# Attention's operands: loads two or three units ahead, splits one unit later, four load slots

## The chip, the cores and the metric

The kernel runs on one core of a Trainium2 chip. The metric is the device time of one execution in microseconds (us); the median of several runs is given. The engines are PE (TensorE, matrix products), ACT (ScalarE), DVE (VectorE), POOL (GpSimd) and SP (SyncE), which issues all the DMA transfers here. Each engine takes its instructions in the order in which they stand in its queue; an instruction that waits holds all behind it.

## The reference

Two layers of a diffusion backbone over 1024 latent tokens and 256 context tokens. Each layer projects the normed input once, runs latent attention and a two-way gated delta rule side by side, joins both in one output projection, and ends in a squared-ReLU MLP. The change lies in attention, whose core is this:

```python
def mla_attend(q, k, v):
    ...
    def block(qi):
        s = jnp.einsum('bqhd,bkhd->bhqk', qi, k).astype(jnp.float32) * scale
        p = jax.nn.softmax(s, axis=-1).astype(v.dtype)
        return jnp.einsum('bhqk,bkhd->bqhd', p, v)

    attn_l = mla_attend(q, jnp.concatenate([kc, k], axis=1), jnp.concatenate([vc, v], axis=1))
    ...
    if not last:
        attn_c = mla_attend(qc, kc, vc)
```

There are 8 heads with 96 query and key columns and 64 value columns, all in float32. The context tokens' own attention is left out in the last layer.

## The kernel before, in words

Each layer has three stages. Stage 1 projects the input and writes queries, keys and values to DRAM (tensors qd, kd, vd). Stage 2 runs attention and the delta rule together. Stage 3 does the output projection and the MLP. To keep float32 precision, products are made of three: every operand is held as a high part (the value rounded to the engine's float32r format) and an exact remainder, and `mm3` (lines 313 to 315) adds high by high, low by high and high by low.

In stage 2 the work of attention is cut into units of 256 queries of one head: the context block (b = 0, one unit, first layer only), and two latent blocks (b = 1, 2) of two units each, called half 0 and 1. Layer 0 has 40 units and layer 1 has 32; one more step drains the last unit. `front` makes a unit's scores, takes them out of their bank with their maximum (DVE, `keep`), and applies the exponential (ACT, line 896, two per unit). It then sends the reciprocal sums through DRAM (rinv out, rb back). `back` transposes the exponentials (PE, pt), splits them into high part ph (ACT, line 927) and remainder pl (DVE, line 928), multiplies them by the values (PE, o, line 916), scales the result (POOL, ob, waiting for rb) and stores it (cat). The unit i's front and the unit i - 1's back are interleaved by the string PATTERN, and steps of the delta rule (products g, line 984, with their loads v, kt, kT, qT, QK, A and B) are laid between units.

A head's operands come by `parts`: for each chunk of 512 columns a load from DRAM into a slot raw (SP, line 831; three slots), a cast to the high part (ACT, line 832: kh, v, qh), and a subtraction for the remainder (line 834: on DVE for the first loads of a layer, on POOL after that). The keys of a head are three chunks, the values two, the queries of a block one. `load` and `loadq` are called at the start of the front that first needs the values.

The order of the instructions on each engine is not that of the source: a scheduler fixes it when the program is built. It takes the instructions by priority, which is the order of the source, as soon as its own model of time says that their operands and slots are ready. So a later head's load may be drawn ahead of earlier work. `tc.issue_after(ins)` holds those instructions of a block that run on the engine of `ins` behind `ins` in that engine's queue.

Of the kernel before, what the change touches and what calls it, by code (L numbers as in the profile page):

```python
# [46 lines left out]
# columns of the constant table  # L47
C_ID, C_M0, C_M1, C_ONE, C_W = 0, 128, 256, 384, 512
# and the part of it that is needed once
# [24 lines left out]
def host_layout(inp):  # L74
# [16 lines left out]
    # tiles of output columns: q 4, k 4, v 4, misc, kv_a, q_a 2, z 4  # L91
# [4 lines left out]
    # the rotary columns: first halves of all heads, second halves of all heads  # L96
# [19 lines left out]
class K:  # L116
# [13 lines left out]
    # ---------------------------------------------------------------- set-up  # L130
# [24 lines left out]
    def side(self, l):  # L155
        """The ends of the memory for the features and weights, and for the rest; layers swap them."""
        self.msd, self.osd = ("right", "left") if l % 2 else ("left", "right")
# [8 lines left out]
    def start(self, mmp, pjp, tpp, stp):  # L166
        """Modulation of the first norm, the first norm, and the first two output tiles, as the features come."""
        nc, io, cst = self.nc, self.io, self.cst
        with ExitStack() as es:
# [12 lines left out]
            # features and weights are queued behind the modulation's weights  # L182
# [73 lines left out]
    # ---------------------------------------------------------------- adaLN  # L256
    def ada_tile(self, l, m, vs, sp, width, other=()):
        """Column m of the modulation; the vectors in other go by way of Pool and ACT and want their sum()."""
# [17 lines left out]
    def ada_sum(self, l, v, m):  # L276
        """Eight columns that came by way of Pool and ACT, from their halves and the bias."""
# [4 lines left out]
    def load_sc(self, sp):  # L282
        """silu(c) and silu(c_ctx) on all partitions."""
        self.sc_b = []
        for v in range(2):
            t = sp.tile([P, D], F32, name=f"scr{v}")
            self.nc.sync.dma_start(t, self.scd[v].partition_broadcast(P))
            self.sc_b.append(t)

    def gain(self, l, j, vs):  # L290
        """(1 + scale) * gain of norm j."""
# [5 lines left out]
    # ---------------------------------------------------------------- weights  # L297
    def wload(self, src):
        """A [128, 1024] weight from DRAM as its float32r high part and exact remainder."""
# [17 lines left out]
    # ---------------------------------------------------------------- norms  # L317
    def rstat(self, sq, n, denom, stp, rbp=None):
        """rsqrt(mean + eps) over partitions of the [128, n] squares (list added), as PSUM [128, n] rows."""
# [17 lines left out]
    def norm_mod(self, xs, rb, b, l, which, pool):  # L337
        """Modulated RMSNorm of block b (8 tiles [128, n]) into the high and low parts of h."""
# [22 lines left out]
    # ---------------------------------------------------------------- stage 1  # L361
    def stage1(self, l, last):
        """Input projection, short conv, gates, chunk preparation, latent attention's projections."""
# [8 lines left out]
        # the solves may go on into the next stage  # L372
# [59 lines left out]
        def conv_tile(m, blocks, it=None):  # L432
            """Projection, short conv, twice the silu."""
# [65 lines left out]
        def first():  # L499
            """The first two output tiles, side by side, while the norm goes on."""  # L500
# [72 lines left out]
    def kpe(self, l, it, sp, tpp):  # L573
        """Rotary key part of all heads, and the gate columns by token."""
# [40 lines left out]
    def gates(self, l, stp):  # L615
        """Per-token scalars of both directions, [128 tokens, direction, tile, head]."""
# [45 lines left out]
        # the squares are of twice the features  # L662
# [24 lines left out]
    # ---- latent attention's low-rank parts  # L687
# [6 lines left out]
    def lowrank(self, raw, b, g, sp, stp):  # L694
        """RMSNorm of the low-rank features of block b, as high and low parts."""
# [27 lines left out]
    def kv_proj(self, l, raw, sp, mmp, stp):  # L723
        """Keys (but for the rotary part) and values of all heads, to DRAM as high and low parts."""
# [20 lines left out]
    def q_proj(self, l, raw, sp, mmp, stp):  # L745
# [3 lines left out]
        # the scale of the scores  # L749
# [31 lines left out]
    # ---------------------------------------------------------------- stage 2  # L781
    def stage2(self, l, last):
        dr = self.dr
        es = ExitStack()
        # what the first scores need, and then the first steps, lies where the stage before ends first
# [706 lines left out]
```

## Time and profile before

| | |
|---|---|
| median of 3 runs | 3950.51 us (3946.8 to 3952.6) |
| span of the profiled execution, first to last instruction | 3929.9 us |
| PE busy | 3517.4 us (90% of the span) |
| DVE busy | 2134.2 us (54%) |
| POOL busy | 1516.0 us (39%) |
| ACT busy | 1459.3 us (37%) |
| mean granted TensorE clock | 0.937 of full speed |

The profile shows one execution. Busy time is the time in which an engine executes an instruction; the sum over engines is larger than the span, since they work side by side. An engine that is idle waits for a releaser, which the profile names. SP's issues are not counted as busy time; its waits are listed on request.

### The profile page before, as it was taken

What the parts mean: (1) busy time and instruction counts of PE and PEld (TensorE: products, weight loads), DVE (VectorE), ACT (ScalarE), POOL (GpSimd) and SP (SyncE); (2) the same over time, 40 slices, a digit from 0 to 9 for tenths busy, and PEclk for the clock granted to TensorE, in tenths of its full rate; (3) what the DMA queues carried; (4) which work ended last, traced back from release to release, by engine and by line L of the source; (5) the groups of instructions that cost most, each with busy time, mean ns of one, the idle gap of its engine ahead of it and who ended that gap; (6) DMA issues with size and microseconds to landing.
All of it is one profiled execution on the core that took longest, in us unless ns stands there. A gap on an engine that the chain in (4) does not pass through costs nothing.

```text
span 3929.9 us, 52618 instructions
## 1 busy us (share of the span) xinstructions
PE 3517.4 (90%) x19001; PEld 2992.1 (76%) x19001; DVE 2134.2 (54%) x4080; ACT 1459.3 (37%) x3156; POOL 1516.0 (39%) x1358
## 2 busy tenths in 40 slices
PE   8789977887887898999999978888889899999998
PEld 4668766787776777888888757767788788888887
DVE  5157855565769995333333627776667533333334
ACT  4334355565633111121112524336666531222122
POOL 3124864433354232232223313675533352333232
PEclk8899987898998899999999979989899899999999
DMA  5343465535353352111111334454653511111111
GB/s 186 91 136 116 139 149 94 112 93 95 77 199 102 129 180 81 43 44 38 38 33 43 102 94 132 144 147 109 125 101 81 132 57 46 52 51 49 44 54 54
DMA packets 335892, 372.52 MB, mean 95 GB/s; under 512 B 126849, under 2 KB 226577, under 8 KB 333969
## 3 DMA queue, kind: packets, MB, share of 16 engines
q1 hardware_dynamic: 335632, 369.18, 34.3%
q8 instruction: 149, 2.44, 0.3%
q14 instruction: 111, 0.90, 0.1%
HBM read 280.65 MB, written 88.42 MB: 94 GB/s over the span
## 4 chain that ended last, share of the span: by engine, by line
PE 57%; DVE 13%; DMA 12%; issue 5%; ACT 4%; POOL 3%; SPq 1%; POOLq 0%; DVEq 0%; ACTq 0%
PE f2ps L313 6%; PE f2ps L314 6%; PE f2ps L315 6%; PE fps L314 6%; PE fps L315 6%; PE fps L313 6%; DVE adaj L272 3%; DMA raw<-kd 3%; PE g L984 3%; PE o L916 3%; PE pt L924 2%; DVE cacc L444 2%; DVE A L1427 2%; DMA rinv<-rinv 2%; DMA adaw<-w_adaT 1%
## 5 line engine op out<-in xcount | busy, mean ns | idle before, releaser
L308 POOL TENSOR_TENSOR wlo<-wraw,whi 128x1024 fp32r<-128x1024 f32 (+1 forms) x190 | 462.3, 2441 | 1217.8 <-ACT whi L307 1217.8
L1304 DVE SCALAR_TENSOR_TENSOR x<-f2ps,mod,x 128x512 f32<-128x512 f32 (+1 forms) x648 | 440.9, 689 | 353.3 <-PE f2ps L315 353.1
L307 ACT CAST whi<-wraw 128x1024 fp32r<-128x1024 f32 (+1 forms) x190 | 195.6, 1046 | 1008.0 <-PE f2ps L314 692.7
L313 PE MATMUL f2ps<-ah,whi 128*128 128x512 f32 (+1 forms) x1296 | 474.4, 371 | 31.4 <-DVE x L1304 27.2
L314 PE MATMUL f2ps<-al,whi 128*128 128x512 f32 (+1 forms) x1296 | 478.5, 370 | 0.8 <-DVE al L1293 0.8
L313 PE MATMUL fps<-hh,whi 128*128 128x512 f32 (+1 forms) x1288 | 471.3, 368 | 8.8 <-ACT hh L351 8.8
L315 PE MATMUL f2ps<-ah,wlo 128*128 128x512 f32 (+1 forms) x1296 | 477.4, 369 | 0.0
L314 PE MATMUL fps<-hl,whi 128*128 128x512 f32 (+1 forms) x1288 | 474.1, 368 | 0.0
L315 PE MATMUL fps<-hh,wlo 128*128 128x512 f32 (+1 forms) x1288 | 472.9, 368 | 0.0
L1293 DVE TENSOR_TENSOR al<-relu,ah 128x256 fp32r<-128x256 f32 (+1 forms) x161 | 111.5, 699 | 512.9 <-POOL relu L1292 512.9
L313 PE MATMUL mm<-hh,whi 128*128 128x512 f32 (+1 forms) x880 | 333.1, 380 | 35.0 <-ACT craw L430 22.1
L314 PE MATMUL mm<-hl,whi 128*128 128x512 f32 (+1 forms) x880 | 331.4, 377 | 3.6 <-DVE hl L352 2.1
L315 PE MATMUL mm<-hh,wlo 128*128 128x512 f32 (+1 forms) x880 | 327.6, 374 | 0.8 <-POOL wlo L308 0.8
L928 DVE TENSOR_TENSOR pl<-pt,ph 128x512 fp32r<-128x512 f32 x328 | 222.2, 686 | 194.7 <-ACT ph L927 182.1
L313 PEld LDWEIGHTS f2ps<-ah,whi 128*128 128x128 f32 x1296 | 248.2, 192 | 74.4 <-DVE x L1304 29.9
L313 PEld LDWEIGHTS fps<-hh,whi 128*128 128x128 f32 x1288 | 243.7, 190 | 49.1 <-ACT hh L351 9.1
L314 PEld LDWEIGHTS f2ps<-al,whi 128*128 128x128 f32 x1296 | 248.7, 192 | 40.7 <-DVE al L1293 1.0
L315 PEld LDWEIGHTS f2ps<-ah,wlo 128*128 128x128 f32 x1296 | 248.4, 192 | 40.1
L314 PEld LDWEIGHTS fps<-hl,whi 128*128 128x128 f32 x1288 | 244.0, 189 | 40.1 <-POOL hl L357 0.3
L315 PEld LDWEIGHTS fps<-hh,wlo 128*128 128x128 f32 x1288 | 243.9, 189 | 39.8
L924 PE MATMUL pt<-ctab,p 128*128 128x128 f32 x1312 | 219.9, 287 | 32.9 <-ACT p L896 12.7
L1292 POOL TENSOR_TENSOR relu<-relu 128x256 f32<-128x256 f32 (+1 forms) x161 | 159.5, 996 | 225.2 <-ACT ah L1291 209.7
(287 smaller groups left out, 7520.6 us busy)
## 6 DMA issues: line engine op xcount, KB each, us to landing
wraw<-w_ff SPq DMA_DIRECT2D x128, 512.0 KB
adaw<-w_adaT SPq DMA_DIRECT2D x160, 256.0 KB
wraw<-w_in SPq DMA_DIRECT2D x40, 512.0 KB
QK<-QK SPq DMA_DIRECT2D x72, 256.0 KB
A<-A SPq DMA_DIRECT2D x40, 256.0 KB
v<-vtd SPq DMA_DIRECT2D x40, 256.0 KB
kt<-ktd SPq DMA_DIRECT2D x40, 256.0 KB
kT<-kTd SPq DMA_DIRECT2D x36, 256.0 KB
```

Of the source, the lines that this page charges most:

```text
L272: nc.vector.tensor_tensor_reduce(out=j, in0=w, in1=self.sc_b[v][:, s], op0=ALU.mult, op1=ALU.add, scale=1.0, scalar=acc if i else self.bad ...
L307: nc.scalar.copy(hi[:, :n], raw[:, :n])
L308: nc.gpsimd.tensor_tensor(lo[:, :n], raw[:, :n], hi[:, :n].bitcast(F32), op=ALU.subtract)
L313: then(mm(ps, lhsT=lh, rhs=rh, start=start, stop=False))
L314: then(mm(ps, lhsT=lh, rhs=rl, start=False, stop=False))
L315: then(mm(ps, lhsT=ll, rhs=rh, start=False, stop=stop))
L916: nc.tensor.matmul(o, lhsT=v[:, k, :], rhs=x[:, j, :], start=k == 0 and i == 0, stop=k == nkt - 1 and i == 1)
L924: self.mark = nc.tensor.transpose(tp[:, j, i * P:(i + 1) * P], pp[i][:, (k0 + j) * P:(k0 + j + 1) * P], self.ident)
L928: nc.vector.tensor_tensor(pl, tp, ph.bitcast(F32), op=ALU.subtract)
L984: nc.tensor.matmul(ps[:, h, :], lhsT=lhs[:, h, :], rhs=rhs[:, h, :], start=True, stop=True)
L1292: nc.gpsimd.tensor_tensor(r[:, :n], r[:, :n], r[:, :n], op=ALU.mult)
L1304: nc.vector.scalar_tensor_tensor(xs, ps[:, :n], g2, xs, op0=ALU.mult, op1=ALU.add)
```

## The change

Fetching and splitting are taken apart. `fetch` issues the loads and returns a function `split` that does the casts and subtractions. A table, `plan`, says in which unit each fetch is made: keys three units ahead of the head's first unit, values two units ahead, queries of a block two units ahead of its first unit. `prepare`, called at the start of each unit's front, first traces the fetches of that unit and then the splits of what was fetched in the unit before, held by `issue_after` behind that earlier unit's last exponential on ACT. In the first unit, what is due before it is fetched and split at once. The slots raw are four instead of three. (The diff also takes comments out of the whole file; those lines are left out here. The list `keys` moves up unchanged.)

```diff
-        def parts(hi, lo, src):
+        self.amark = None
+
+        def fetch(hi, lo, src):
             p, m = src.shape[0], src.shape[1]
             w = 1 if len(src.shape) == 2 else src.shape[2]
+            got = []
             for c in range(0, m, 512 // w):
                 e = min(m, c + 512 // w)
-                raw = ap1.tile([P, 512], F32, tag="raw", name="raw", bufs=3)[:p, :(e - c) * w]
+                raw = ap1.tile([P, 512], F32, tag="raw", name="raw", bufs=4)[:p, :(e - c) * w]
                 if w > 1:
                     raw = raw.rearrange("p (t n) -> p t n", n=w)
                 nc.sync.dma_start(raw, src[:, c:e])
-                nc.scalar.copy(hi[:, c:e], raw)
-                eng = nc.gpsimd if len(cur) > 3 else nc.vector
-                eng.tensor_tensor(lo[:, c:e], raw, hi[:, c:e].bitcast(F32), op=ALU.subtract)
+                got.append((raw, slice(c, e)))
+
+            def split():
+                for raw, c in got:
+                    nc.scalar.copy(hi[:, c], raw)
+                    eng = nc.gpsimd if len(cur) > 3 else nc.vector
+                    eng.tensor_tensor(lo[:, c], raw, hi[:, c].bitcast(F32), op=ALU.subtract)
+
+            return split
...
+        plan = {}
+        for h in range(H_A):
+            i = min(j for j, k in enumerate(keys) if k[0] == h)
+            plan.setdefault(i - 3, []).append((fetchk, h))
+            plan.setdefault(i - 2, []).append((fetchv, h))
+        for i, k in enumerate(keys):
+            if k[2] == 0:
+                plan.setdefault(i - 2, []).append((fetchq, k[0], k[1]))
+        wait = []
+
+        def prepare(i):
+            if i == 0:
+                for j in sorted(plan):
+                    if j < 0:
+                        for f, *a in plan[j]:
+                            f(*a)()
+            todo, wait[:] = list(wait), [f(*a) for f, *a in plan.get(i, [])]
+            if todo:
+                with self.tc.issue_after(self.amark.ins):
+                    for x in todo:
+                        x()
...
         def front(h, b, half):
-            if (h, b) not in cur:
-                loadq(h, b)
-            if h not in cur:
-                load(h)
+            prepare(keys.index((h, b, half)))
...
-                nc.scalar.activation(pp[i][:, :nk], pp[i][:, :nk], AF.Exp, bias=mn[:, i:i + 1], accum_out=sm[:, i:i + 1])
+                self.amark = nc.scalar.activation(pp[i][:, :nk], pp[i][:, :nk], AF.Exp, bias=mn[:, i:i + 1],
+                                                  accum_out=sm[:, i:i + 1])
```

The scheduler's order shows what becomes of it. On ACT, layer 0, the casts of head 2's keys (kh_6012) stood like this before, among the transposed exponentials (ph) and the two exponentials (p) of head 1's context unit:

```order
L832 CAST kh_6012<-raw_6014 96x512
L896 ACTIVATE p_5318,sm_5315<-p_5318,mn_5317 128x256
L896 ACTIVATE p_5319,sm_5315<-p_5319,mn_5317 128x256
L1014 COPY U64_4377<-B1_4367 32x4x32 x4
L927 CAST ph_5334<-pt_5329 128x512
```

The other two casts of these keys stood ten rows further on, with ph between them. The first cast stood ahead of the unit's exponentials, so that they wait for the load too.

Now head 2's keys (kh_5483) stand behind the second exponential of head 1's unit b = 1, half 1 (p_5497), three in a row:

```order
L926 ACTIVATE p_5496,sm_5493<-p_5496,mn_5495 128x1280
L1497 COPY both_3272<-both_3272 128x32x32
L958 CAST ph_5546<-pt_5541 128x512
L958 CAST ph_5564<-pt_5559 128x512
L926 ACTIVATE p_5497,sm_5493<-p_5497,mn_5495 128x1280
L839 CAST kh_5483<-raw_5485 96x512
L839 CAST kh_5483<-raw_5487 96x512
L839 CAST kh_5483<-raw_5489 96x256
L958 CAST ph_5584<-pt_5579 128x512
```

The casts moved some two units later, and the exponentials of the unit in progress now stand ahead of all three.

On SP, the loads of head 2's keys (kd) and values (vd) stood in one run before, around the stores of the reciprocal sums (rinv) of head 0's last unit and head 1's first:

```order
L902 DMA rinv0_0_2_1_5268<-rinv_5266 128x2x1
L831 DMA raw_6014<-kd_0_507 96x512
L1053 DMA kt_6203<-ktd_0_504 128x512
L1053 DMA QK_5612<-QK0_1_9_2899 128x512
L902 DMA rinv0_1_0_0_5366<-rinv_5364 128x2x1
L831 DMA raw_6018<-kd_0_507 96x512
L1053 DMA kt_6215<-ktd_0_504 128x512
L831 DMA raw_6022<-kd_0_507 96x256
L904 DMA rb_5270<-rinv0_0_2_1_5268 64x256
L942 DMA cat0_0_2_4351<-ob_5282 64x256
L831 DMA raw_6027<-vd_0_509 128x512
L831 DMA raw_6031<-vd_0_509 128x128
```

Now the key loads (raw_5485, raw_5487, raw_5489) stand in nearly the same place, the first two a little earlier, and their casts stand two units later. The second value load and the next two query loads stand behind the rinv store of head 1's unit b = 1, half 1:

```order
L933 DMA rinv0_1_1_1_5590<-rinv_5588 128x2x1
L1483 DMA both_3352<-A0_1_2_2610 32x32x32
L834 DMA raw_5787<-vd_0_509 128x128
L834 DMA raw_5791<-qd_0_508 96x256
L834 DMA raw_5916<-qd_0_508 96x512
L1083 DMA v_6203<-vtd_0_505 128x512
```

The first two of them are cast behind the second exponential of the next unit, the third one unit after that.

## Rows read from the trace of the kernel before

**Rows 1.** The page's head, and the lines of the chain that ended last.

```profile
span 3929.9 us, 52618 instructions
...
PE f2ps L313 6%; PE f2ps L314 6%; PE f2ps L315 6%; PE fps L314 6%; PE fps L315 6%; PE fps L313 6%; DVE adaj L272 3%; DMA raw<-kd 3%; PE g L984 3%; PE o L916 3%; PE pt L924 2%; DVE cacc L444 2%; DVE A L1427 2%; DMA rinv<-rinv 2%; DMA adaw<-w_adaT 1%
```

**Rows 2.** Windows: length, busy time (instructions) of PE, PEld, DVE, ACT, POOL; clock, DMA, GB/s.

```profile
560.00:1060.00 500.00, 399.11 (x2795) 363.91 (x2793) 307.78 (x895) 292.62 (x725) 202.21 (x257) 0.88 0.49 98
1000.00:1050.00 50.00, 48.66 (x359) 44.30 (x358) 41.21 (x125) 34.27 (x85) 16.80 (x17) 1.00 0.26 54
...
2600.00:3090.00 490.00, 425.52 (x3004) 383.44 (x3002) 331.98 (x940) 316.23 (x748) 228.89 (x306) 0.91 0.49 109
2700.00:2750.00 50.00, 46.12 (x380) 42.71 (x378) 33.95 (x90) 36.22 (x93) 32.94 (x50) 1.00 0.59 133
2950.00:3000.00 50.00, 48.34 (x346) 43.80 (x345) 36.86 (x111) 32.81 (x80) 17.50 (x18) 0.96 0.34 91
```

**Rows 3.** Waits of ACT, 560 to 1060 us: total us, times, longest.

```profile
ACT kh L832 <- DMA raw<-kd: 83.5, 18, 10.1
...
ACT blb L1455 <- DMA both<-A: 9.5, 1, 9.5
ACT v L832 <- DMA raw<-vd: 8.7, 2, 7.5
```

**Rows 4.** Waits of ACT, 2600 to 3090 us.

```profile
ACT kh L832 <- DMA raw<-kd: 59.6, 16, 9.3
...
ACT v L832 <- DMA raw<-vd: 7.2, 2, 5.3
```

**Rows 5.** Timeline of PE: start, duration, instruction, idle before it and releaser.

```profile
591.89 0.47 PE L1026 MATMUL g<-B,Y 128*64 128x64 f32 x2 [4.89 <-ACT Y L1022]
...
776.44 0.80 PE L916 MATMUL o<-ph,v 128*128 128x256 f32 x2 [11.00 <-ACT ph L927]
...
979.96 1.33 PE L1042 MATMUL g<-U,Y 128*128 128x64 f32 x5 [4.89 <-ACT Y L1038]
...
2623.56 0.47 PE L924 MATMUL pt<-ctab,p 128*128 128x128 f32 x1 [2.06 <-ACT p L896]
...
3004.99 0.79 PE L916 MATMUL o<-ph,v 128*128 128x256 f32 x2 [6.36 <-ACT ph L927]
```

**Rows 6.** Timeline of ACT, casts of kh.

```profile
613.48 0.62 ACT L832 CAST kh<-raw 96x512 fp32r<-96x512 f32 x1 [8.54 <-DMA raw<-kd]
...
625.43 0.62 ACT L832 CAST kh<-raw 96x512 fp32r<-96x512 f32 x1 [6.18 <-DMA raw<-kd]
...
774.66 0.62 ACT L832 CAST kh<-raw 96x512 fp32r<-96x512 f32 x1 [10.10 <-DMA raw<-kd]
...
790.27 0.40 ACT L832 CAST kh<-raw 96x256 fp32r<-96x256 f32 x1 [9.55 <-DMA raw<-kd]
```

**Rows 7.** Timeline of SP's queue, two issues of raw<-kd.

```profile
615.78 0.42 SPq L831 DMA_DIRECT2D raw<-kd  x1
...
780.64 0.44 SPq L831 DMA_DIRECT2D raw<-kd  x1
```

**Rows 8.** Waits of SP's queue, 560 to 1060 us.

```profile
SPq L904 <- DMA rinv<-rinv: 123.2, 22, 8.3
...
SPq L831 <- POOL kl L834: 12.1, 10, 2.0
```

**Rows 9.** Timeline of PE, two products of 512 columns.

```profile
632.66 0.63 PE L315 MATMUL S<-kh,ql 96*128 96x512 f32 x1
...
633.45 0.39 PE L313 MATMUL S<-kh,qh 96*128 96x512 f32 x1
```

**Rows 10.** Instructions on the tile raw: ns shortest/median/longest, first and last start.

```profile
L832 ACT CAST kh<-raw x48: 399/617/624, 499.5 to 3005.4; 96x512 fp32r<-96x512 f32 x32, 96x256 fp32r<-96x256 f32 x16
L834 POOL TENSOR_TENSOR kl<-raw,kh x42: 718/1262/1308, 518.2 to 3006.3; 96x512 fp32r<-96x512 f32 x28, 96x256 fp32r<-96x256 f32 x14
...
L832 ACT CAST v<-raw x32: 282/459/622, 509.3 to 3019.9; 128x512 fp32r<-128x512 f32 x16, 128x128 fp32r<-128x128 f32 x16
```

More of the change, by code (lines that the diff above doesn't have):

```diff
@@ L831, in parts @@
                 nc.sync.dma_start(raw, src[:, c:e])
-                nc.scalar.copy(hi[:, c:e], raw)
-                eng = nc.gpsimd if len(cur) > 3 else nc.vector
-                eng.tensor_tensor(lo[:, c:e], raw, hi[:, c:e].bitcast(F32), op=ALU.subtract)
-        def load(h):
-            t = {}
-            for nm in ("kh", "kl"):
-                t[nm] = (ap2 if h % 2 else ap1).tile([DQK, NT], F32R, tag=nm, name=nm)
-            parts(t["kh"], t["kl"], self.kd[h])
-            t["v"] = v = ap2.tile([P, NTT, P], F32R, tag="v", name="v", bufs=2)
-            parts(v[:, :, 0:64], v[:, :, 64:], self.vd[h])
-            cur[h] = t
@@ L845, in loadq, with fetchk @@
-        def loadq(h, b):
+                got.append((raw, slice(c, e)))
[5 more added lines that the diff above has]
+            return split
+        def fetchk(h):
+            k = [(ap2 if h % 2 else ap1).tile([DQK, NT], F32R, tag=nm, name=nm) for nm in ("kh", "kl")]
+            cur[h] = {"kh": k[0], "kl": k[1]}
+            return fetch(*k, self.kd[h])
@@ L846, in loadq, with fetchv, fetchq @@
+        def fetchv(h):
+            cur[h]["v"] = v = ap2.tile([P, NTT, P], F32R, tag="v", name="v", bufs=2)
+            return fetch(v[:, :, 0:64], v[:, :, 64:], self.vd[h])
+        def fetchq(h, b):
             t0, n = BLOCKS[b]
             cur[h, b] = r = [ap1.tile([DQK, 512], F32R, tag=nm, name=nm, bufs=2) for nm in ("qh", "ql")]
-            parts(r[0][:, :n], r[1][:, :n], self.qd[h, :, t0:t0 + n])
+            return fetch(r[0][:, :n], r[1][:, :n], self.qd[h, :, t0:t0 + n])
+        keys = [(h, b, half) for h in range(H_A) for b in ([1, 2] if last else [0, 1, 2]) for half in range(1 if b == 0 else 2)]
@@ L942, in back @@
             nc.sync.dma_start(self.cat[h // 2, b][(h % 2) * 64:(h % 2) * 64 + 64, q0:q0 + 256], ob[0:64])
-        keys = [(h, b, half) for h in range(H_A) for b in ([1, 2] if last else [0, 1, 2]) for half in range(1 if b == 0 else 2)]
         units = []
```

## The prediction

> **What bounds the kernel now.** I read the page's chain first: matrix multiplies (PE) carry most of it, but one load stands among its ten longest lines, the load of attention's keys, raw<-kd, with 3% of the span, about 120 us [rows 1]. All of that load's uses lie in stage 2, so I went to the windows of that stage. Layer 0 runs it roughly from 560 to 1060 us and layer 1 from 2600 to 3090. PE is busy for 399.11 of 500 us and 425.52 of 490 us there, at a mean granted clock of 0.88 and 0.91; it stands idle for 165 us in the two together. The same windows show stretches of 50 us without a load in trouble, in which PE is busy for 46 to 49 us at 0.96 to 1.00 [rows 2]. So the stage is bound by PE only part of the time.
>
> The waits of ACT say what stops it. ACT's largest wait is for raw<-kd at the casts of kh: 83.5 us in 18 waits in layer 0, 59.6 us in 16 in layer 1. With the waits for raw<-vd (8.7 and 7.2 us) it is 159 us [rows 3, 4]. ACT takes its instructions in order, and the casts ph of the softmax, which PE's second product needs, stand behind the kh casts. The timelines show the transfer: ACT waits 10.10 us for raw<-kd before the cast at 774.66, and PE's product o at 776.44 has waited 11.00 us for ACT's ph [rows 5, 6]. I set every idle piece of PE of 0.7 us or more in the two windows beside ACT's waits. 25 pieces, from the one before 591.89 (4.89 us) to the one before 979.96 (4.89 us) in layer 0 and from the one before 2623.56 (2.06 us) to the one before 3004.99 (6.36 us) in layer 1, fall while or just after ACT waits for such a load; they add up to 104 us (the ends of each list are in [rows 5]). Two pieces at the start of layer 1's stage, where the first head's loads can't come earlier, are left out.
>
> Why are the loads late? A load issued at 615.78 is used at 625.43, one issued at 780.64 at 790.27: some 9.6 us each [rows 6, 7]. And the issue itself comes late, since SP issues in order and stands 123.2 us in layer 0 for the store rinv to land before it can issue the load rb [rows 8].
>
> **The change, part by part.** Nothing is added or removed: 120 loads, 120 casts on ACT and 120 subtractions before and after, one subtraction moving from DVE to POOL (1.26 us there, off the path). What changes is where a cast stands. The order shows that before, three kh casts stood apart, each among the ph casts and exponentials of a running unit; now all three stand in a row behind the last exponential of a unit, and their loads stand in SP's order more than one unit ahead of them.
>
> *Key casts.* A key load is now issued some two units ahead of its cast. A unit lasts 565 us / 41 = 13.8 us in layer 0 and 490 / 33 = 14.8 us in layer 1 (the stages' lengths by their unit counts). Against 9.6 us from issue to use, two units hide the load with room to spare. I take all of the 104 us as gone; below that, one unit of cover would still do for the key loads.
>
> *The clock.* After an idle piece the granted clock falls to its lower level: the 512-column product at 632.66 lasts 0.63 us and the one at 633.45 lasts 0.39 us [rows 9]. Means of 0.88 and 0.91 make 120 + 88 = 208 us at half rate [rows 2]. If all idle time (165 us) lay inside, 43 us of work ran at half rate and lost 21 us; if PE was as busy there as on average (825 of 990 us), 173 us of work lost 87. I take the middle, 54 us, and the share of the load waits, 104/165: 34 us come back. Ends: 13 and 55.
>
> *The second value load and the first query load.* This is the part that may be late. There are four slots, three keys fill three of them, and the first value load takes the fourth. The next value load and the next query load take the slots of the first two keys, which come free one unit later: behind an exponential, a cast of 0.62 us and a subtraction of 1.26 us on POOL [rows 10], some 2.5 us in all. Their own casts are pinned behind the next unit's last exponential. So they have one unit, about 12.5 us once the stage is shorter, for 2.5 + 9.6 = 12.1 us. On average that fits; sometimes it does not. I take 1 us of waiting for each of 14 heads (seven in each layer; the first head has no predecessor): 14 us. Ends: 0, and 74 us if SP stands a mean rinv wait (123.2 / 22 = 5.6 us) longer in front of them each time (5.3 us x 14).
>
> The Trainium skill (DMA: Bandwidth & Descriptors, "Anatomy of one DMA") fits about 2.0 us plus bytes over 436 GB/s for a DMA, on another issue path than SP's; for the 192 KB of a 96x512 load that is an estimate of 2.5 us. The trace does not agree: some 9.6 us pass from issue to use here. By the page this term would be 0 and the sum 14 us lower.
>
> *Bursts.* Three kh casts take 1.6 us in a row, two v casts and one qh cast about 1.4 us [rows 10]; ph casts queue behind them. Cover is PE's own queue of scores and of delta-rule products. Without it, 14 x 3 = 42 us; with it, nothing. The former casts already stood among the same instructions, so I take a third, 14 us.
>
> *What remains.* 61 us of PE's idle time is not behind these loads: for example ACT waits 9.5 us for the solve's data [rows 3]. The solve on POOL gets no shorter, so a faster stage meets it earlier; 6 us for that, ends 0 and 20.
>
> Sum: 104 + 34 - 14 - 14 - 6 = 104 us. The profiled execution's span is 3929.9 us and the median of the runs 3950.5, 20.6 us more, which lies around the span. 3929.9 - 104 + 20.6 = 3846.5; I say **3847 us**.
>
> **Rivals.**
> *Better: PE's pace without trouble.* At 359 PE instructions in 50 us the 2795 of layer 0 take 389 us; at the mean of 380 and 346 the 3004 of layer 1 take 414 us [rows 2]. That saves 187 us: 3764 us. Against it: waits other than for loads are in that time too. With most of it, a saving over 150 us, about 3785 us. Chance 0.13.
>
> *SP becomes the bound.* A load that waits for POOL to free its slot holds all of SP's queue: rb, the store of the result, and the delta rule's loads behind it. Already SP stands 12.1 us for kl in layer 0 [rows 8]. Three such loads per head at 2.5 to 3 us are some 8 us per head, and delta-rule loads that were early now arrive when needed; at 4 us of PE idle per head, 14 x 4 = 56 us of the saving go: about 3903 us. Chance 0.14. The Trainium skill (the same page and section) says that any semaphore wait happens on the issuing sequencer before dispatch; the trace agrees, by SP's waits of 123.2 and 12.1 us.
>
> *The change does nothing: the idle time moves on to the next wait*, rb or the solve, and PE loses the same. Against it: the undisturbed stretches [rows 2]. 3950 us. Chance 0.05.
>
> *Slower.* The pinned casts of v and qh hold ACT as the kh casts do now. 159 us of waits over 14 heads are 11.4 us per head. If the loads of one head, stuck in SP behind rb, hold ACT for more than that, which means an arrival 23.9 us behind the exponential that frees the slots, the change loses. For that, SP must hold them 11.8 us beyond the 12.1; its longest rinv wait is 8.3 us [rows 8]. At 12.5 us per head: 14 x 1.1 = 15 us, 3965 us. Chance 0.08.
>
> **How the numbers follow.** Forecast (saving 60 to 150 us) 0.60, better 0.13, SP-bound 0.14, nothing 0.05, slower 0.08. 0.2% of the time, 7.9 us, is about what a measurement of this kernel can tell from no change. Faster: 0.60 + 0.13 + 0.14 = 0.87; the same 0.05; slower 0.08. The range leaves out the slower and the unchanged case and the far end of the better one: 3785 to 3915 us; the likeliest case's own range is 3800 to 3890.
>
> **What the profile will show.** If right: ACT's waits for raw<-kd fall from 143 us to under 15; PE's idle in stage 2 falls from 165 us to 60 to 90; its clock there rises to 0.94 or more; stage 2 is some 60 us shorter in layer 0 and 45 in layer 1, and stages 1 and 3 keep their lengths. The term for the second value load shows as ACT waits for raw<-vd or raw<-qd: 5 to 30 us in all. Wrong would be: those waits above 80 us (the slot wait or SP), or PE waiting for the delta rule's operands where it waited for ph.

## The result, and the profile after

The changed kernel takes 3899.1 us (median of 4 runs, 3888.6 to 3909.3); the kernel before, run beside it on the same chip, 3951.6 us (3946.8 to 3958.4). The ratio is 0.9869, with a 95% interval from 0.9852 to 0.9885: 52 us saved (45 to 58), where 104 were forecast. The time lies in the range given, and the waits for keys went as forecast, but half of the saving is missing.

The head and the chain of the profile after [rows 1 are those of before]:

```profile
span 3907.5 us, 52623 instructions
...
PE f2ps L313 6%; PE f2ps L314 6%; PE f2ps L315 6%; PE fps L314 6%; PE fps L315 6%; PE fps L313 6%; DVE adaj L272 3%; PE o L947 2%; PE g L1014 2%; DVE A L1457 2%; PE pt L955 2%; DVE cacc L444 2%; DMA adaw<-w_adaT 2%; DMA rinv<-rinv 2%; PE mm L313 1%
```

The key load raw<-kd, 3% before, is gone from the chain; the store rinv, 2% before, is still there. That second name is the one to remember. The windows of stage 2, from the first scores to the first output product, of both layers (columns as in [rows 2]):

```profile
512.00:1075.00 563.00, 456.57 (x3178) 409.62 (x3177) 355.69 (x1022) 348.44 (x846) 249.34 (x327) 0.90 0.56 107
2593.00:3093.00 500.00, 419.18 (x3008) 376.07 (x3007) 332.60 (x934) 321.82 (x757) 232.98 (x308) 0.91 0.60 108
```

PE is still idle for 1063 - 876 = 187 us, and its clock is at 0.90 and 0.91. The waits of ACT in the first window (as in [rows 3]: total us, times, longest):

```profile
ACT v L839 <- DMA raw<-vd: 25.6, 4, 9.5
...
ACT cat L1215 <- DMA craw<-catg: 17.4, 4, 7.2
...
ACT UD L1040 <- DMA B<-B: 13.4, 1, 13.4
...
ACT cat L1215 <- DMA craw<-cat: 11.2, 2, 7.9
ACT blb L1485 <- DMA both<-A: 10.0, 1, 10.0
```

And those in the second window, beside [rows 4]:

```profile
ACT X L1042 <- DMA B<-B: 23.4, 2, 17.2
ACT v L839 <- DMA raw<-vd: 17.3, 4, 13.2
...
ACT whi L307 <- DMA wraw<-w_out: 11.4, 2, 11.0
...
ACT qh L839 <- DMA raw<-qd: 6.4, 6, 3.0
```

No wait for raw<-kd is left in either window. In its place stand other loads: the second value load, the delta rule's B, the solve's data, and the first loads of stage 3 (craw, w_out), whose casts the scheduler draws ahead into stage 2. SP still stands for rinv, from 560 to 1060 us even longer than in [rows 8]:

```profile
SPq L935 <- DMA rinv<-rinv: 150.8, 22, 8.9
```

One late value load in three timelines. First PE (start, duration, instruction, idle before it and releaser):

```profile
2853.51 0.79 PE L947 MATMUL o<-ph,v 128*128 128x256 f32 x2 [13.00 <-ACT ph L958]
```

ACT, on which PE waits, at the splits of the next head's keys and of the values:

```profile
2824.73 1.43 ACT L839 CAST kh<-raw 96x512 fp32r<-96x512 f32 x3
...
2851.34 0.30 ACT L839 CAST v<-raw 128x128 fp32r<-128x128 f32 x1 [13.18 <-DMA raw<-vd]
```

SP's queue, where the load is issued:

```profile
2833.46 0.46 SPq L935 DMA_DIRECT2D rb<-rinv  x1
...
2839.10 0.55 SPq L933 DMA_DIRECT2D rinv<-rinv  x1
2839.75 0.41 SPq L1083 DMA_DIRECT2D kt<-ktd  x1
2840.26 0.38 SPq L834 DMA_DIRECT2D raw<-vd  x1
```

The three key casts run without a wait. The value load, as forecast, is late. It is issued at 2840.26, just behind a store rinv, and takes until 2851.34, 11.1 us for 64 KB.

For the whole of stage 2, I put each idle piece of PE over 0.7 us to the load (or the solve's data) for which ACT was waiting then or up to 3 us before (us, both layers; "other" holds the short pieces too). It is a sorting by time, and an idle piece can have more than one cause. Labels stand for the runs below:

| kernel | span | key | value, query | solve, B | stage 3's casts | other | PE idle | PE busy |
|---|---|---|---|---|---|---|---|---|
| before, the profile shown | 3929.9 | 96 | 10 | 40 | 33 | 22 | 201 | 891 |
| before once more (b_again) | 3972.5 | 123 | 10 | 47 | 43 | 21 | 243 | 887 |
| changed | 3907.5 | 0 | 41 | 62 | 44 | 40 | 187 | 876 |
| changed once more (a_again) | 3918.7 | 0 | 52 | 60 | 48 | 40 | 199 | 877 |
| before, four slots (e_before4) | 3919.3 | 77 | 7 | 41 | 40 | 30 | 195 | 881 |
| changed, three slots (e_slots3) | 3929.0 | 23 | 36 | 55 | 50 | 39 | 202 | 886 |
| before, sums by PE (e_b_rb_pe) | 3766.5 | 5 | 0 | 10 | 6 | 43 | 64 | 864 |
| changed, sums by PE (e_rb_pe) | 3768.6 | 0 | 0 | 14 | 7 | 43 | 65 | 866 |

### The profile page after: what moved, and what is told of

The parts are those of the page before. It is cut to its first block, busy times and chain, and to the rows that moved or that the text cites. A ratio compares the mean times of both kernels' runs of the same rounds, so it can differ in the third digit from the quotient of the medians.

```text
span 3907.5 us, 52623 instructions
## 1 busy us (share of the span) xinstructions
PE 3506.5 (90%) x19001; PEld 2981.0 (76%) x19001; DVE 2138.5 (55%) x4079; ACT 1457.7 (37%) x3156; POOL 1518.2 (39%) x1359
## 2 busy tenths in 40 slices
DMA packets 335894, 372.55 MB, mean 95 GB/s; under 512 B 126848, under 2 KB 226576, under 8 KB 333968
## 4 chain that ended last, share of the span: by engine, by line
PE 54%; DMA 15%; DVE 13%; issue 5%; ACT 4%; POOL 3%; SPq 1%; DVEq 0%; POOLq 0%; ACTq 0%
PE f2ps L313 6%; PE f2ps L314 6%; PE f2ps L315 6%; PE fps L314 6%; PE fps L315 6%; PE fps L313 6%; DVE adaj L272 3%; PE o L947 2%; PE g L1014 2%; DVE A L1457 2%; PE pt L955 2%; DVE cacc L444 2%; DMA adaw<-w_adaT 2%; DMA rinv<-rinv 2%; PE mm L313 1%
```

## The experiments

Every ratio is to the kernel before on the same chip; its median there was between 3968 and 3977 us.

### The two kernels again

No edit.

> The kernel before once more, unchanged, for a second profile. If the first profile (span 3929.9 us) was an uncommonly short execution, the span comes out at 3940 to 3955 us, and PE's idle time in stage 2 is some 15 to 25 us above the 200 us of the first profile (512 to 1099 and 2612 to 3118 us). If the difference of some 20 us between span and time lies around the span, the span comes out near 3930 us again.

Measured: 3974.2 us with a span of 3972.5. So 1.7 us lie around the span, not 20.6: the execution that the prediction had was itself some 20 us quicker than the timed runs. The span here is longer than either expectation, on a chip whose median for this kernel is 3973 us; PE is idle for 42 us more than in the first profile, 27 of them beside raw<-kd, for which ACT waits 108.3 and 59.4 us here.

> The changed kernel unchanged, so that the others of this chip can be set beside it. If the chip only scales all times, the ratio to the kernel before is again 0.985 to 0.989. If the ratio depends on how long this chip's loads take, it may be anywhere from 0.980 to 0.990; keys one unit earlier stood at 0.983 and the load rb without its wait at 0.977 on the chip on which the kernel before took 3973 us.

Measured: 0.9852 (0.9826 to 0.9877), 3913.1 us. The change is worth the same on this chip.

### Parts of the change

```diff
-                raw = ap1.tile([P, 512], F32, tag="raw", name="raw", bufs=3)[:p, :(e - c) * w]
+                raw = ap1.tile([P, 512], F32, tag="raw", name="raw", bufs=4)[:p, :(e - c) * w]
```

The slot alone, in the kernel before:

> The kernel before with four load slots in place of three and nothing else. My theory: the loads were late because SP issued them when they were already due, not for lack of a slot, so ACT's waits for raw<-kd stay above 100 us in the two layers together and the ratio to the kernel before is 0.997 to 1.002. Rival: the fourth slot alone lets the loads go out earlier; then the waits for raw<-kd fall below 70 us and the ratio is 0.985 to 0.992.

Measured: 0.9877 (0.9842 to 0.9911), with 53.8 and 40.9 us of waits for raw<-kd. My theory fell: the slot alone gives four fifths of the gain, though 95 us of the key waits stay. The same edit taken back in the changed kernel (bufs=3):

> The changed kernel with three load slots in place of four. The kernel before with a fourth slot and nothing else gave 0.988, so my theory is now that the slots carry most of the gain: without the fourth, three keys fill all slots, the first value load too has to wait for a key's cast, ACT's waits for raw<-vd and raw<-qd grow from about 60 us to over 90, and the ratio to the kernel before is 0.993 or more, perhaps above 1. Rival: the loads ahead and the casts later carry it by themselves; then the ratio stays at 0.984 to 0.989.

Measured: 0.9874 (0.9843 to 0.9905). This theory fell too. Either part gives almost what both give.

```diff
-                with self.tc.issue_after(self.amark.ins):
-                    for x in todo:
-                        x()
+                for x in todo:
+                    x()
```

> The changed kernel without the hold behind the last exponential: the scheduler may draw the casts forward again. Theory: the hold is what keeps ACT from standing for a key load; without it ACT waits for raw<-kd again for 60 us or more, and the time goes back to 3920 to 3960 us. Rival: the earlier loads and the fourth slot do it alone; then ACT's waits for raw<-kd stay below 20 us and the time is 3880 to 3905 us.

Measured: 0.9854 (0.9839 to 0.9869). ACT's waits for raw<-kd come back to 47.2 and 12.3 us, and the time stays. The hold, and with it the exact place of the casts, on which the prediction's main term rested, is not what saves time.

### The next waits, one by one and together

```diff
-            plan.setdefault(i - 3, []).append((fetchk, h))
+            plan.setdefault(i - 4, []).append((fetchk, h))
```

> The changed kernel with the keys fetched four units ahead of the head instead of three, and so split one unit earlier; the second value load and the next query load then get their slots a unit earlier and have two units until their casts. Theory slots-and-queue: these loads are what is late (ACT waited some 50 us for raw<-vd and raw<-qd in the changed kernel, 43 us of it for raw<-vd); those waits fall below 12 us and the time falls by 25 to 45 us against the changed kernel, to 3855 to 3875 us. Rival, other waits: PE's idle time is now that of the solve's blocks (B) and of stage 3's first loads; then the waits for raw<-vd go and the time stays within 10 us of 3899.

Measured: 0.9826 (0.9811 to 0.9841). PE's idle time beside value and query loads falls to 4 us, but all of its idle time in stage 2 is still 185 us: 54 beside stage 3's casts, 52 beside the solve and B, 63 beside neither. Some 10 us are won; the rest of the idle time now stands beside other waits.

```diff
-                nc.scalar.copy(ph, tp)
+                self.phmark = nc.scalar.copy(ph, tp)
...
-                nc.scalar.copy(hi, raw)
+                with self.tc.issue_after(self.phmark.ins):
+                    nc.scalar.copy(hi, raw)
```

The cast of w_out in `wload` is held in the same way.

> The changed kernel, with the first casts of stage 3 on ACT (those of cat<-craw and of the weights w_out) put in order behind the last cast ph of attention; the loads are issued as before. In the profile after, 44 us of PE's idle time in the end of stage 2 lie beside ACT's waits at these casts. If they are what took back a good part of the gain, that idle time falls below 10 us and the time falls by 20 us or more against the changed kernel on the same chip (0.5%). Rival: the data that these casts wait for come no earlier, so the wait only moves behind the stage's end, before PE's first products ops, and the time stays within 8 us (0.2%).

Measured: 0.9820 (0.9788 to 0.9852), 3904.7 us, 8 us under the changed kernel there. Stage 2 is 56 us shorter in the two layers together (539.1 and 481.1 us for 568.2 and 508.5), but from the first output product to the MLP's first it takes 166 us in layer 0 for 142 in the changed kernel. The rival holds for the most part: the data come no earlier.

```diff
-        for j in range(31):
+        for j in range(31 if bi == 0 else 4):
```

> The changed kernel, with 4 of the 31 steps of the second and third triangular solve on POOL (27 steps of each are left out, so the inverses are not the reference's). In the profile after, 62 us of PE's idle time lie beside ACT's waits for the solve and its data (both, blb, B). If POOL's solve is what these waits end on, at least 30 us of that idle time go and the time falls by 25 us or more (0.6%) against the changed kernel on the same chip. Rival: the loads of B are late in SP's queue or for another reason; then the idle time beside them stays above 45 us and the time falls by less than 10 us.

Measured: 0.9809 (0.9783 to 0.9836), 15 us less. Of the 60 us beside the solve and B, 51 stay: POOL's solve is not what most of them end on. Whether the loads of B are late in SP's queue, as the rival has it, is not tried by itself.

```diff
-            nc.sync.dma_start(rb[0:64], rd.rearrange("i p -> (i p)").partition_broadcast(64))
+            nc.sync.dma_start(rb[0:64], self.io["ctab"][0, 0:256].partition_broadcast(64))
```

> The changed kernel with the load rb taken from a constant table in DRAM, so that SP never waits for the store rinv to land; the store is still made, and the division by the row sums is left out of the result's value. Theory queue: SP stands 271 us behind rb for rinv in the two stages, and this is what makes the second value load late; ACT's waits for raw<-vd and raw<-qd fall below 15 us, those for the blocks B fall too, and the time falls to 3830 to 3870 us. Rival slots: the loads are late because their slots come free too late; then these waits stay above 35 us and the time stays at 3885 us or more.

Measured: 0.9770 (0.9746 to 0.9794), though ACT's waits for raw<-vd and raw<-qd stay at 47 us. All four edits together:

> The changed kernel with everything that took a wait away, at once: keys one unit earlier, the load rb from a table instead of the reciprocals (the division by the row sums is left out), the first casts of stage 3 behind attention's last ph, and 4 of 31 steps in the second and third solve (27 steps of each are left out). By themselves they stood at about 10, 32, 8 and 15 us under the changed kernel. If the losses are separate, they add up: 65 us, ratio 0.969, near the 3847 us that I had forecast, scaled to this chip. Rival: they stand in for one another, and with one gone the next is met; then less than 40 us come back and the ratio is 0.975 or more.

Measured: 0.9672 (0.9644 to 0.9701), 3839.8 us. The losses add up: 0.969 lies inside the interval.

The same without the change, in the kernel before:

> The kernel before with all that the run with everything removed had, except the change itself and the keys one unit earlier: rb from a table, stage 3's first casts behind the last ph, 4 of 31 steps in the second and third solve (the division and 27 steps of each solve are left out). With the change these gave 0.967. If the change is worth more once the other waits are out of its way, about what I forecast (2.6%), this stands at 0.985 or more. If it is worth the same 1.3 to 1.5% (and the keys 0.25%) with or without them, it stands at 0.981 to 0.985. Rival: with SP free the loads come in time even in the kernel before; then it stands at 0.977 or less and the change is worth under 1% here.

Measured: 0.9817 (0.9796 to 0.9837). The change and the earlier keys are worth 0.9672 / 0.9817 = 0.985 on top of it, as much as alone. So the missing half is not waiting behind these waits.

### SP's standing, or the store itself

The table in place of rinv, in the kernel before:

> The kernel before with the load rb from a table in place of the reciprocals (the division by the row sums is left out) and nothing else: three slots, loads where they were. The prediction said that the key loads are issued late because SP stands for rinv. By that, ACT's waits for raw<-kd fall from about 165 us to below 100 here, and the ratio to the kernel before is 0.990 or less. Rival: the loads are late for want of a slot alone; then those waits stay above 130 us and the ratio is 0.993 or more.

Measured: 0.9857 (0.9837 to 0.9877), the time of the theory with nearly the waits of the rival. ACT's waits for raw<-kd in stage 2 of the two layers, in the kernel before (b_again):

```profile
ACT kh L832 <- DMA raw<-kd: 108.3, 17, 13.0
...
ACT kh L832 <- DMA raw<-kd: 59.4, 13, 12.4
```

And in this run:

```profile
ACT kh L832 <- DMA raw<-kd: 88.8, 18, 10.2
...
ACT kh L832 <- DMA raw<-kd: 40.3, 10, 10.1
```

SP no longer waits for rinv at rb, yet most of the key waits stay. A key load of this run, first its issue in the timeline of SP's queue, with the load rb before it and the next one:

```profile
777.63 0.48 SPq L904 DMA_DIRECT2D rb<-ctab  x1
...
782.44 0.38 SPq L902 DMA_DIRECT2D rinv<-rinv  x1
782.92 0.41 SPq L831 DMA_DIRECT2D raw<-kd  x1
...
798.55 0.48 SPq L904 DMA_DIRECT2D rb<-ctab  x1
```

Its cast in the timeline of ACT:

```profile
792.20 0.41 ACT L832 CAST kh<-raw 96x256 fp32r<-96x256 f32 x1 [5.53 <-DMA raw<-kd]
```

The load is issued at once, and still needs 9.3 us for 96 KB. Here it is the transfer that is slow, not the issue, and no load rb is issued between 777.63 and 798.55: of the two it is the store rinv that stands just ahead of it. The windows of the 10 us behind the store and of the 4 us after them (columns as in [rows 2]):

```profile
783.00:793.00 10.00, 10.00 (x66) 9.25 (x65) 4.10 (x12) 2.47 (x6) 1.59 (x2) 0.82 0.41 25
793.00:797.00 4.00, 3.36 (x24) 2.93 (x24) 3.88 (x14) 1.82 (x6) 1.75 (x3) 1.00 0.72 232
```

All transfers of the core together move 25 GB/s in the first stretch and 232 in the second. The store's own packets are not what fills these 10 us: in the trace, 272 packets of 4 bytes start within the first of them and last 8 to 9 ns each. So I went back to the unchanged kernel (b_again) for two loads of that same size, one issued 0.6 us behind a store rinv, the other 10 us behind one and after a load rb, which waits for such a store to land. SP's queue:

```profile
790.09 0.54 SPq L902 DMA_DIRECT2D rinv<-rinv  x1
790.73 0.43 SPq L831 DMA_DIRECT2D raw<-kd  x1
...
850.01 0.42 SPq L902 DMA_DIRECT2D rinv<-rinv  x1
859.03 0.47 SPq L904 DMA_DIRECT2D rb<-rinv  x1
859.85 0.48 SPq L942 DMA_DIRECT2D cat<-ob  x1
860.45 0.50 SPq L831 DMA_DIRECT2D raw<-kd  x1
```

Their casts on ACT:

```profile
800.69 0.41 ACT L832 CAST kh<-raw 96x256 fp32r<-96x256 f32 x1 [10.06 <-DMA raw<-kd]
...
862.78 0.40 ACT L832 CAST kh<-raw 96x256 fp32r<-96x256 f32 x1 [2.02 <-DMA raw<-kd]
```

10.0 us and 2.3 us. Of the loads raw issued after 540 us for which ACT waited in this run, the 15 that were issued within 6 us behind a store rinv took 8.7 to 18.3 us from issue to cast, 10.3 in the middle; the other 22 took 1.9 to 9.4, 3.5 in the middle. In the profile of before on which the prediction rests it is the same: 9.4 us for 15, 3.6 for 24. Both loads of [rows 7] are of the first kind. A load rb just ahead does not do this: the four that were issued within 2 us behind one, and not so close behind a store, took 2.3 to 5.1 us. But slow transfers are only half of the matter. Without the first head of layer 1, the loads close behind a store hold 90 of these 178 us of waits, and the others 88: those took 4.6 us in the middle, and much of their lateness was a late issue.

The store rinv writes 128x2 single values, transposed (`rd.rearrange("i p -> p i")`), and SP stands until it has landed. Does it help to let another engine stand for it?

```diff
-            nc.sync.dma_start(rb[0:64], rd.rearrange("i p -> (i p)").partition_broadcast(64))
+            nc.gpsimd.dma_start(rb[0:64], rd.rearrange("i p -> (i p)").partition_broadcast(64))
```

> The changed kernel, computing all that it did, with the load rb issued by POOL in place of SP. SP then no longer stands for rinv (150 and 120 us in the profile after), but POOL does. If SP's standing is what makes the delta rule's, the solve's and the value loads late, most of the 32 us that the table in place of rinv gave come back: ratio 0.976 to 0.980. Rival: POOL's standing holds the subtractions and the solve, so that the slots come free later and B is ready later; then the ratio is 0.985 or more.

Measured: 0.9881 (0.9855 to 0.9907). With keys one unit earlier and stage 3's casts held:

> The changed kernel, computing all that it did, with three edits: keys one unit earlier, stage 3's first casts behind attention's last ph, and rb issued by POOL. If the three gains (10, 8 and up to 32 us) are separate, the ratio to the kernel before is 0.972 to 0.977, the fastest that computes everything. Rival: POOL's standing costs what SP's gives back; then it is 0.979 to 0.983.

Measured: 0.9873 (0.9846 to 0.9900), worse than even the rival. In the first of the two runs POOL now stands for rinv for 136.9 us in layer 0. The store and what it does to other transfers are still there.

Now rinv is taken out of memory altogether. First by way of the transposes (to make room, the tile oh has one buffer in place of two):

```diff
+            dg = ap2.tile([P, 2, P], F32, tag="rb", name="dg", bufs=2)
+            for i in range(2):
+                nc.vector.tensor_scalar(dg[:, i, :], self.ident, r[:, i:i + 1], None, op0=ALU.mult)
...
-                        self.mark = nc.tensor.transpose(tp[:, j, i * P:(i + 1) * P], pp[i][:, (k0 + j) * P:(k0 + j + 1) * P], self.ident)
+                        self.mark = nc.tensor.matmul(tp[:, j, i * P:(i + 1) * P], lhsT=pp[i][:, (k0 + j) * P:(k0 + j + 1) * P], rhs=dg[:, i, :], start=True, stop=True)
```

> The changed kernel, computing all that it did, with the division moved: the transposes of p become products with a diagonal matrix that holds the reciprocals (two 128x128 products of DVE per unit), and the store rinv, the load rb and POOL's product are gone. Products of this form and size last 287 ns in the profile after and the transposes 289 ns, so PE pays nothing. If SP's standing for rinv and its queue cost the 32 us that the table gave, the ratio is 0.972 to 0.979. Rival: the transposes now wait for the diagonal, a reciprocal and two products behind the exponential, 72 times about 0.5 us, and DVE has some 30 us more; then it is 0.982 or more.

Measured: 0.9868 (0.9849 to 0.9887). With the two other edits:

> The run with the diagonal, with keys one unit earlier and stage 3's first casts behind the last ph; all of the computation is there. If the three are separate (32, 10 and 8 us) the ratio is 0.970 to 0.975, faster than the change by over 1%. Rival: the diagonal's wait costs what SP's gives back; then it is 0.979 or more.

Measured: 0.9891 (0.9872 to 0.9909). The transposes' group among PE's lines says why (layer 0; xcount, busy us and mean ns of one). The changed kernel:

```profile
L955 PE MATMUL pt<-ctab,p 128*128 128x128 f32 x672 | 113.0, 289 | 36.7 <-ACT p L926 14.4 <-DVE pl L959 14.2 <-DVE p L908 8.0
```

The run e_diag:

```profile
L954 PE MATMUL pt<-dg,p 128*128 128x128 f32 x1344 | 187.9, 281 | 32.8 <-DVE dg L934 31.3 <-DVE p L908 1.0 <-DVE pl L958 0.3
```

Twice the instructions: the product of p and dg, both float32, stands as two matrix instructions here, the transpose as one. PE is busy for 991 us in stage 2 instead of 876. But PE's idle time fell from 187 to 85 us, and no wait for a load raw was left. So, at a small price in PE's work:

```diff
+            rb = psA.tile([P, 2, 256], F32, tag="a", name="rb")
+            for i in range(2):
+                nc.tensor.transpose(rb[0:64, 0, i * P:(i + 1) * P], r[:, i:i + 1].to_broadcast([P, 64]), self.ident)
...
-            nc.gpsimd.tensor_tensor(ob[0:64], ob[0:64], rb[0:64], op=ALU.mult)
+            nc.vector.tensor_tensor(ob[0:64], ob[0:64], rb[0:64, 0, :], op=ALU.mult)
```

The tile rd, its store and the load rb are gone. (The units are 72, not the 74 of the expectation.)

> The changed kernel, computing all that it did, with the reciprocals brought along the queries by PE: two transposes of a broadcast column per unit, and the product with them on DVE; the store rinv, the load rb and POOL's product are gone, as with the diagonal. There PE's idle time in stage 2 fell from 187 to 85 us but its work grew by 115 us, since every product of two 32-bit operands takes two passes and a transpose takes one. Here PE gets 2 x 0.28 us x 74 units = 41 us of work. If SP's standing is what keeps the loads late, 70 to 100 us of idle time go again and the time falls by 30 to 60 us under the changed kernel: ratio 0.970 to 0.978. Rival: the idle time went only because PE was slower and so covered the loads; then it falls by 40 us or less and the ratio is 0.983 or more.

Measured: **0.9501** (0.9479 to 0.9524), 3770.7 us, far more than my theory asked: not only SP's standing is gone. And the same edit in the kernel before:

> The kernel before with the same edit (reciprocals by PE, no rinv or rb on SP) and without the change. If the waits for raw<-kd come from SP standing for rinv, they fall below 60 us without any load being moved and the ratio is within 0.004 of the changed kernel's with this edit, so the change is then worth less than 0.4%. If they come from the slots and the order of the loads, they stay above 110 us, and the change is worth 1.2 to 1.5% on top of this edit.

Measured: **0.9492** (0.9469 to 0.9515), 3768.3 us. The change is worth nothing on top of it. The windows of stage 2, first in the kernel before (b_again):

```profile
514.00:1127.50 613.50, 462.97 (x3177) 416.25 (x3176) 351.29 (x1021) 347.90 (x843) 245.76 (x321) 0.87 0.51 98
2642.00:3159.20 517.20, 424.33 (x3009) 382.72 (x3008) 332.58 (x937) 323.22 (x756) 232.06 (x306) 0.89 0.51 106
```

And in this run:

```profile
512.00:992.00 480.00, 443.32 (x3257) 395.70 (x3256) 366.64 (x1060) 348.55 (x844) 218.52 (x283) 0.97 0.42 119
2505.20:2953.00 447.80, 420.92 (x3074) 378.65 (x3073) 341.57 (x968) 322.68 (x757) 211.26 (x275) 0.97 0.42 119
```

ACT's waits for loads raw in the first window of this run:

```profile
ACT kh L832 <- DMA raw<-kd: 4.3, 7, 1.3
ACT v L832 <- DMA raw<-vd: 2.3, 2, 1.3
```

Two key loads in the timeline of SP's queue, the second of the size shown above:

```profile
773.58 2.85 SPq L831 DMA_DIRECT2D raw<-kd  x2
```

The cast of the second on ACT:

```profile
778.08 0.41 ACT L832 CAST kh<-raw 96x256 fp32r<-96x256 f32 x1 [1.25 <-DMA raw<-kd]
```

The loads are called where they were called before, in three slots. The second of the two is now there in 2.0 us, PE idles for 64 us instead of 243, its clock is at 0.97 for 0.87 and 0.89, and the DMA engines move more (119 GB/s for 98 and 106) in a smaller share of their time (0.42 for 0.51). Part 3 of the page (packets, MB, share of 16 engines' span) of the changed kernel:

```profile
q1 hardware_dynamic: 335632, 369.18, 36.5%
```

And of this run:

```profile
q1 hardware_dynamic: 310288, 364.38, 32.1%
```

The store rinv and the load rb were 25,344 packets, 352 for each of the 72 units. By the two shares all packets together took 0.365 x 16 x 3907.5 - 0.321 x 16 x 3766.5 = 3475 us less of one DMA engine. That is not the time of the packets that went. In the traces, the packets of 4 bytes took 9 ns each in both kernels, so the 20,700 or so of them that went account for 0.2 ms. The 79,488 packets of 2 KB, as many in both, took 131 ns each with the store and 104 without, which is 2.1 ms. The store's price is paid by the transfers beside it.

One part of the edit is not apart from the rest: POOL's product, which waited 49.0 us for rb in layer 0 of b_again, moved to DVE as well, and no run moves it alone. It cannot shorten a load that is already issued, but POOL's subtractions free the slots, so some of the 5% may be its own. The table in place of rinv took that wait and SP's away and left the store, for 1.4%.

## Why the saving was half of the forecast

Over the two layers, from b_again to a_again, stage 2 became 54 us shorter, and the spans 53.8. By the prediction's terms, with what the table above and PE's busy time gave for each:

- *Key casts*, 104 us forecast: 123 us of PE's idle time are gone. Right, and more than forecast.
- *The second value load and the first query load*, 14 us: 42 us (10 to 52). This is the step that failed: "1 us of waiting for each of 14 heads". It counted 2.5 us until the slot is free, an issue right then, and 9.6 us for the load. The 9.6 us held: the seven second value loads for which ACT waited in the changed kernel took 8.1 to 11.7 us. The issue right then did not: these loads went out 0 to 13.4 us after their slot was free. The upper end of the term, 74 us, was priced for such a wait.
- *The clock*, 34 us: PE's busy time fell by 10 us. The 34 were for all 104 us of idle time; only 44 went in sum (243 to 199), and the clock rose from 0.87 and 0.89 to 0.88 and 0.91.
- *Bursts*, 14 us: "other" rose by 19 us. That these are the bursts is not shown.
- *What remains*, 6 us: solve and B cost 13 us more, stage 3's casts 5 us.

In sum -123 + 42 - 10 + 19 + 18 = -54.

The 13.4 us are those of the case shown under the result. POOL is done with the first key's slot, which the late value load takes, at 2826.9:

```profile
2825.60 1.28 POOL L841 TENSOR_TENSOR kl<-raw,kh 96x512 fp32r<-96x512 f32 x1
```

SP issues that load at 2840.26. Until 2833.46 it stands at rb for a store rinv to land, and ten other transfers come first in its order, the next store rinv among them.

Of the signs, the waits for raw<-kd (0), the unchanged other stages and the range came true; PE's idle time (187 us, not 60 to 90), its clock and the waits for value and query loads (51 us, not 5 to 30) did not. Nor did the split by layer: stage 2 became 45 us shorter in layer 0 and 9 in layer 1, not 60 and 45. The 20.6 us "around the span" were not there.

Behind the sum stands a reading: "some 9.6 us each" was taken as what a load costs, to be hidden. It was what a load costs behind a store rinv, and the same store made SP stand. The prediction set the Trainium skill's fit (DMA: Bandwidth & Descriptors, "Anatomy of one DMA"), an estimate of 2.5 us for such a load, beside the 9.6 us of the trace and left the gap unexplained. (By the fit the saving would have been 14 us more: its "sum 14 us lower" holds for the time alone.) With the store gone, the loads for which ACT still waits in stage 2 take 1.9 to 4.6 us, so the fit was near, and the gap was the finding. The same page of the Trainium skill ("Rules for kernel authors") says that a transfer with a strided last dimension becomes one descriptor per element. The trace agrees: 20,735 of the packets that went were under 512 B (126848 to 106113 by the page of the profile), 288 a unit, for a store of 256 values. That page of the Trainium skill also says ("Queues, rings and completion order") that each DMA engine takes descriptors in ring order. The trace agrees in that the loads issued behind a store are the late ones, but the order does not explain the length: the store's packets had started within 1 us, and the load took 9.3. What holds the transfers up for the rest of that time is not shown.

Of the rivals, the time of "SP becomes the bound" (3903 us) came nearest, by luck: its reason was a load that waits for POOL to free its slot, and the case above waits for rinv. "The idle time moves on to the next wait" was more than half of the truth: of the 123 us, 79 came back beside other waits or beside none. SP's standing for rinv at rb, which the prediction gave as the reason for late loads, is a lesser part of that lateness: without it in the kernel before, three quarters of ACT's key waits stay (129 of 168 us), though it too saves 1.4%.

Why a fourth slot, earlier loads and no wait at rb each save about 50 us is not settled. The first two together, which are the change, save hardly more; the table on top of them brings 2.3%. They do not take away the same waits. Of the 90 us of ACT's waits for loads close behind a store and 88 us for others (b_again), the fourth slot leaves 11 and 89, the change 57 and 4, the table in place of rinv 76 and 61. With the reciprocals by PE in the kernel before, 11 us are left in all. What is shown is that both kinds go with the store and the load rb, and that the change is worth nothing then. That the store slows the loads behind it without the load rb is seen in the run with the table; a store of another shape was not tried.

## What to carry to other kernels

Where a load is late, look first at how long it takes from issue to landing, and sort such times by what was issued just ahead of it: two clusters, here 3.5 and 10.3 us, can mean that another transfer is in its way. A transfer of single values is small in bytes and in its own packets' time, and can still cost the others most; moving a few hundred values across partitions by PE took 0.54 us of PE a unit here, and the edit saved 5%. Work on slots and order hid this delay from one load, and the next one met it.

## What the hardware showed that I had not expected

- A store of 128x2 single values takes about 10 us to land, and loads issued close behind it take some 7 us longer than others, while the DMA engines' mean share is only 0.51. In the case shown the core's transfers moved 25 GB/s in these 10 us and 232 right after.
- A product of two float32 operands of 128x128 stands as two matrix instructions of 281 ns in the mean, a transpose of the same size as one of 289 ns.
- Two transposes of a column broadcast to 64 columns, 272 ns each, lay 256 values along the free dimension on 64 partitions.
